# Values and gates in the heads take all 16 K tiles by Strassen

## The chip, the cores and the metric

The program runs on one core of a Trainium2 chip. The metric is the device time of one execution in microseconds. A core has TensorE (PE in the rows; its weight loads are PEld), VectorE (DVE), ScalarE (ACT), GpSimd (POOL) and SyncE (SP), which here issues the loads of weights.

## The reference

Two layers of a decoder trunk are applied to 512 prompt rows and 8 sample rows, 520 columns in all once the activations are transposed. The projection `h @ w_in` is where the change lies:

```python
h = rmsnorm(x, norm_g)
z = h @ w_in                                   # 2048 x 8192
b_c, c_c, x_c, g_c, q, k, v, g_r = split_projection(z)
...
o, new_S = retention(q, k, v, ret_S, retention_log_gamma())   # 4 heads of 256
y_ret = (groupnorm(o) * gn_g) * jax.nn.silu(g_r)
x = x + jnp.concatenate([y_conv, y_ret], axis=-1) @ w_out
x = x + jax.nn.sigmoid(x @ w_pg) * (p_i @ w_ple)
```

## The kernel before

Activations lie transposed: 16 K tiles of 128 rows by 520 columns, in two halves of 260. Every product is made in three matmuls of the fp32r type (`mm3`, lines 247 to 249): operands and weights are each split into a high and a low part, and high x high, high x low and low x high are added up. For weights `split_w` makes the high part on ScalarE (line 229) and the low part on VectorE (line 230); they lie in a ring of 60 tiles of 128 columns (`split`).

Output tiles are made in pairs, `pair(x, src, m, n)`, two tiles of 128 rows by 520 columns. A pair is the four blocks (two weight rows by two column halves), and `strassen` makes it with seven products instead of eight. It takes the first s of the 16 K tiles in two groups of s/2: the even tiles and the odd ones. Products use either the weights w11, w21, w22, w12 themselves or sums of them. The four sums are formed in place in the raw ring on VectorE (`add`, line 319), in chunks of up to 4 tiles (`CHA = 4`), and every product's weights are split in chunks of up to 4 tiles (`CHS = 4`). Loads of whole groups are line 312. The sums on the operands' side are made once for a layer and kept in slots (`x.sums`); a pair of s tiles uses the first s/2 of them.

K tiles beyond s are done plainly, at the end of the pair, in the loop `for i, j in chunks(s, KT)`: they are loaded and split by `parts` (loads at line 222), and each takes four products. With s = 14 there are two such tiles; with s = 16 none. Accumulators are PSUM banks `ps_g`, five in all. With s = 14 a pair takes a, b, c, d; with s = 16 the bank c is not taken, and one product is copied to the result's slot at once (`c = banks.get() if s < KT else None`). Copies and sums out of the banks are line 307, on ScalarE and VectorE; the copies `ps_g<-ps_g` go from bank to bank, two in a pair of 14 and one in a pair of 16.

The numbers s stand in tables, one entry per pair: `HEADS` (four pairs per head: queries q, keys k, values v, gates g), `CONVS` (16 pairs of the convolution branch, 14 in the first two and the last, else 16), `OUT_ROWS` and `GATES` for the two later products. In layer 0 the first head's q and k pairs are made elsewhere, so `HEADS[0][2:]` begins with its v pair. The host packs each pair's weights in the order that its s asks for (`k_order`), even tiles, odd tiles, the rest.

The work of a head's retention (scores, state, normalization) is cut in steps and put into the middle and the ends of the next head's pairs (`later`, `aside`), and the sample rows' state updates (`sample`) too. Those, the rope of q and k (lines 752 to 757) and the gates' silu are VectorE and ScalarE work beside the pairs. The final order on each engine is set by a scheduler that goes by a timeline of its own (`schedule_with_timeline_sim=True`) and by the priorities in the code.

Of the kernel before, what the change touches and what calls it, by code (L numbers as in the profile page):

```python
# [49 lines left out]
EARLY = 6  # L50


HEADS = [[0, 0, 0, 8] + [14] * 12, [0] + [14] * 15]
CONVS = [[14] * 2 + [16] * 13 + [14]] * 2
OUT_ROWS = [[0, 8, 16, 16, 16, 16, 16, 0]] * 2

# [135 lines left out]
def trunk_kernel(  # L192
# [370 lines left out]
    def norm_g(l, k):  # L563
        return vec[:, 16 * l + k : 16 * l + k + 1]
# [97 lines left out]
    def from_dram(src):  # L662
        def load(k):
            t = get()
            SIDE.dma_start(t, src[k])
            return t

        return load

    xs = []  # L670
    X = Operands(HEADS[0][2:] + CONVS[0], from_dram(xT), gain=lambda k: norm_g(0, k))
    X.todo = [t for t in ((i, False, True) for i in range(max(X.rows) // 2))]
# [43 lines left out]
    for l in range(DEPTH):  # L716
# [456 lines left out]
        if not tail:  # L1173
            X = Operands(HEADS[l + 1] + CONVS[l + 1], next_in, RESERVE_NEXT, gain=lambda k, l=l: norm_g(l + 1, k))
        for m in range(0, KT - tail, 2):
# [303 lines left out]
```

## Time and profile before

| | |
|---|---|
| time, median of 3 runs | 2168.64 us (2165.82 to 2170.73) |
| the profiled execution | 2169.1 us |
| its span | 2167.3 us |
| TensorE busy | 2147.8 us (99%), 17861 matmuls |
| VectorE busy | 1896.1 us (87%), 3849 instructions |
| ScalarE busy | 1264.5 us (58%), 2647 instructions |

The span is the profiled execution without 1.8 us around it. Matmuls overlap, so the length of one is longer than the time from one start to the next. On a line of a table of stretches, "(x..)" is the number of an engine's instructions in the stretch. The heads of layer 0 lie before about 381 us, the convolution pairs up to about 730 us; the heads of layer 1 lie between about 1110 and 1473 us, the convolution pairs up to about 1796 us. Within the heads 239 to 287 us holds a v and a g pair of layer 0 (head 2), 287 to 331 us a q and a k pair (head 3); 1379 to 1426 us holds a q and a k pair of layer 1 (head 3), 1426 to 1473 us the v and the g pair behind it.

### The profile page before, as it was taken

To read this page: it belongs to the slowest core of one execution; us is meant where nothing else is said; L and a number is where in the kernel's file an instruction comes from. 1 tells how busy PE (TensorE), PEld (TensorE's weight loads), DVE (VectorE), ACT (ScalarE), POOL (GpSimd) and SP (SyncE) were. 2 spreads that over 40 slices of the span, in tenths; PEclk is the share of its full clock that TensorE was granted. 3 is DMA by queue.
4 is the path that set the end of the run, shared out by engine and by line. 5 is a ranking of instruction groups with operands and counts; after the bars stand their busy time and mean duration, and the time that the engine had idled before them with its cause. 6 is when DMAs were issued, how large, how long until landed. Compare 5 with 4: busy or idle time off the path is not lost. (4 is left out here: it accounts for less than half of the span.)

```text
span 2167.3 us, 48178 instructions
## 1 busy us (share of the span) xinstructions
PE 2147.8 (99%) x17861; PEld 2142.1 (99%) x17861; DVE 1896.1 (87%) x3849; ACT 1264.5 (58%) x2647; POOL 430.6 (20%) x746
## 2 busy tenths in 40 slices
PE   9999999999999999999999999999999999999998
PEld 9999999999999999999999999999999999999998
DVE  8889988998999987987997988989999998879884
ACT  8656655565555655655765655565645555456565
POOL 2313222211001211200212222231111022011011
PEclk9999999999999999999999999999999999999999
DMA  8555565545543745645645566664464355566455
GB/s 288 171 175 197 181 217 184 178 157 175 158 129 118 238 156 187 215 154 160 215 144 175 172 213 191 189 209 170 151 182 149 120 158 202 176 207 200 128 164 198
DMA packets 182861, 387.31 MB, mean 179 GB/s; under 512 B 25888, under 2 KB 56352, under 8 KB 182624
## 3 DMA queue, kind: packets, MB, share of 16 engines
q1 hardware_dynamic: 128704, 212.98, 31.6%
q0 software_dynamic: 53056, 169.84, 23.8%
q8 instruction: 140, 2.29, 0.4%
q10 hardware_dynamic: 864, 1.39, 0.2%
q14 instruction: 97, 0.79, 0.1%
HBM read 318.96 MB, written 65.15 MB: 177 GB/s over the span
## 5 line engine op out<-in xcount | busy, mean ns | idle before, releaser
L247 PE MATMUL ps_g<-slot,split 128*128 128x260 f32 x5465 | 1531.6, 284 | 7.2 <-ACT slot L307 2.9
L248 PE MATMUL ps_g<-slot,split 128*128 128x260 f32 x5465 | 1534.3, 282 | 0.3 <-DVE slot L555 0.3
L249 PE MATMUL ps_g<-slot,split 128*128 128x260 f32 x5461 | 1519.9, 283 | 0.5 <-DVE split L230 0.5
L229 ACT ACTIVATE split<-raw 128x512 fp32r<-128x512 f32 (+2 forms) x1347 | 777.3, 596 | 583.1 <-DVE raw L319 213.2
L247 PEld LDWEIGHTS ps_g<-slot,split 128*128 128x128 f32 x5465 | 1024.0, 188 | 10.1 <-ACT slot L307 3.7
L248 PEld LDWEIGHTS ps_g<-slot,split 128*128 128x128 f32 x5465 | 1028.5, 188 | 0.5 <-DVE slot L555 0.5
L249 PEld LDWEIGHTS ps_g<-slot,split 128*128 128x128 f32 x5461 | 1019.8, 188 | 1.0 <-DVE split L230 1.0
L230 DVE TENSOR_TENSOR split<-raw,split 128x512 fp32r<-128x512 f32 (+2 forms) x1346 | 849.2, 652 | 172.5 <-PE ps_g L248 85.4
L319 DVE TENSOR_TENSOR raw<-raw 128x512 f32<-128x512 f32 (+1 forms) x660 | 428.9, 660 | 32.5 <-DMA raw<-wi 23.7
L307 ACT ACTIVATE slot<-ps_g 128x260 f32<-128x260 f32 x336 | 127.4, 381 | 140.6 <-PE ps_g L249 122.7
L551 ACT ACTIVATE slot<-slot 128x520 fp32r<-128x520 f32 (+1 forms) x212 | 109.2, 562 | 46.6 <-DVE slot L414 11.1
L552 DVE TENSOR_TENSOR slot<-slot,slot 128x520 fp32r<-128x520 f32 (+1 forms) x212 | 124.4, 620 | 4.1 <-ACT slot L551 3.9
L781 POOL DMA_DIRECT2D o_rets<-slot x64 | 35.3, 552 | 351.6 <-DVE slot L780 131.7
L307 DVE TENSOR_TENSOR slot<-ps_g,slot 128x260 f32<-128x260 f32 x168 | 70.9, 424 | 6.0 <-PE ps_g L249 3.7
L869 POOL DMA_DIRECT2D slot<-hs x64 | 46.2, 724 | 118.7 <-DVE split L230 42.7
L814 POOL DMA_DIRECT2D hs<-slot x64 | 35.6, 556 | 139.3 <-DVE slot L755 61.3
L780 DVE SCALAR_TENSOR_TENSOR slot<-slot,vs,slot 128x256 f32<-128x256 f32 x128 | 56.1, 481 | 4.5 <-ACT slot L776 4.3
L746 DVE TENSOR_TENSOR slot<-slot,slot 128x520 f32<-128x520 f32 x80 | 55.8, 698 | 4.7 <-DMA o_rets<-slot 3.7
L770 POOL DMA_DIRECT2D slot<-sret x64 | 35.5, 554 | 114.6 <-ACT split L229 37.3
L1058 POOL DMA_DIRECT2D slot<-x1s x76 | 40.8, 538 | 87.6 <-PE ps_g L249 27.2
L1209 POOL DMA_DIRECT2D x2s<-slot x30 | 16.4, 545 | 201.6 <-DVE slot L1204 200.6
L771 POOL DMA_DIRECT2D slot<-kq x64 | 34.9, 547 | 106.0 <-DVE slot L876 22.2
(217 smaller groups left out, 1733.8 us busy)
## 6 DMA issues: line engine op xcount, KB each, us to landing
raw<-wi SPq DMA_DIRECT2D x377, 256.0 KB, 3.9
raw<-wo SPq DMA_DIRECT2D x128, 256.0 KB, 5.4
raw<-wg SPq DMA_DIRECT2D x122, 256.0 KB, 4.1
raw<-wi SPq DMA_DIRECT2D x136, 192.0 KB, 4.0
slot<-x1s POOLq DMA_DIRECT2D x76, 260.0 KB, 5.1
slot<-sret POOLq DMA_DIRECT2D x64, 256.0 KB, 4.0
hs<-slot POOLq DMA_DIRECT2D x64, 256.0 KB, 4.0
slot<-hs POOLq DMA_DIRECT2D x64, 256.0 KB, 5.2
```

The costliest lines, as they stand in the source:

```text
L229: S.activation(hi, raw, AF.Copy)
L230: V.tensor_tensor(lo, raw, F(hi), SUB)
L247: PE.matmul(out, wh, xh, start=start, stop=False, skip_group_check=more)
L248: PE.matmul(out, wh, xl, start=False, stop=False, skip_group_check=more)
L249: PE.matmul(out, wl, xh, start=False, stop=stop, skip_group_check=more)
L307: fn(*args)
L319: V.tensor_tensor(out[:, n], x[:, n], y[:, n], op)
L551: keep(S.activation(hi, src[:, n], AF.Copy))
L552: V.tensor_tensor(lo, src[:, n], F(hi), SUB)
L746: V.tensor_tensor(out[:, n], v, table[:, n], MUL)
L780: keep(V.scalar_tensor_tensor(st[:, c], k, vs[:, h, e, b : b + 1], st[:, c], MUL, ADD))
L869: SIDE.dma_start(t[:, :512].rearrange("p (m n) -> p m n", m=2), src)
```

## The change

```diff
-HEADS = [[0, 0, 0, 8] + [14] * 12, [0] + [14] * 15]
+HEADS = [[0, 0, 0, 8] + [14, 14, 16, 16] * 3, [0, 14, 16, 16] + [14, 14, 16, 16] * 3]
```

In each group of four entries the first two are q and k, the last two v and g. The v and g pairs of heads 1 to 3 in layer 0 and of all four heads in layer 1 take s = 16 instead of 14: six pairs and eight. Each of them loses the loop over the two remaining tiles and the bank c, and its seven products and four weight sums have 8 tiles instead of 7. Numbers of instructions that differ in the whole program: TensorE 17827 to 17785; VectorE 3851 to 3823 (line 230: 98 splits of 128x384 become 128x512 and 28 of 128x256 go; line 319: 56 sums of 128x384 become 128x512); ScalarE 2655 to 2613 (line 229 as line 230, and 14 bank-to-bank copies go); SP 886 to 858 (28 loads of 128x256 go, 56 of 128x384 become 128x512).

VectorE, layer 0, the start of the same v pair, the difference: `split` and `raw` are weights, the rest is head 0's retention and head 1's rope.

```order
 L757 TENSOR_TENSOR slot_144_1422<-slot_144_1422,slot_164_1701 128x520
-L230 TENSOR_TENSOR split<-raw,split 128x384
+L230 TENSOR_TENSOR split<-raw,split 128x512
 L904 TENSOR_TENSOR slot_167_1850<-ps_s,slot_145_1542 128x512
-L319 TENSOR_TENSOR raw<-raw 128x384
+L319 TENSOR_TENSOR raw<-raw 128x512
 L918 SCALAR_TENSOR_TENSOR slot_173_1873<-ps_vt,r5p,slot_172_1872 128x256
-L230 TENSOR_TENSOR split<-raw,split 128x512
-L319 TENSOR_TENSOR raw<-raw 128x384
+L319 TENSOR_TENSOR raw<-raw 128x512
+L230 TENSOR_TENSOR split<-raw,split 128x512
 L876 TENSOR_TENSOR slot_169_1853<-slot_167_1850,slot_168_1852 128x512
```

Splits and sums of 3 tiles have become 4 tiles wide, and a sum stands before a split where it stood behind it.

TensorE, layer 0, the same v pair towards its end, with buffer numbers: before, `ps_g_2078`, `ps_g_2079` and `ps_g_2080` are its banks b, d and c, and the slots 46 to 49 hold the two remaining tiles.

```order
L248 MATMUL ps_g_2078<-slot44_45_577,split_73 128x260
L249 MATMUL ps_g_2078<-slot43_44_576,split_73 128x260
L247 MATMUL ps_g_2080<-slot46_47_605,split_73 128x260
L248 MATMUL ps_g_2080<-slot46_47_605,split_73 128x260
L249 MATMUL ps_g_2080<-slot46_47_605,split_73 128x260
L247 MATMUL ps_g_2080<-slot47_48_634,split_73 128x260
L248 MATMUL ps_g_2080<-slot48_49_635,split_73 128x260
L249 MATMUL ps_g_2080<-slot47_48_634,split_73 128x260
L247 MATMUL ps_g_2079<-slot45_46_604,split_73 128x260
L248 MATMUL ps_g_2079<-slot45_46_604,split_73 128x260
L249 MATMUL ps_g_2079<-slot45_46_604,split_73 128x260
```

The same pair now, where its fourth product (bank d) ends and the fifth begins; `ps_g_2077` is its bank a, `ps_g_2379` the first bank of the g pair behind it, and `ps_ot` is head 0's retention.

```order
L247 MATMUL ps_g_2079<-slot47_48_634,split_73 128x260
L248 MATMUL ps_g_2079<-slot48_49_635,split_73 128x260
L249 MATMUL ps_g_2079<-slot47_48_634,split_73 128x260
L995 MATMUL ps_ot_2214<-ident_75,slot13_179_2040 128x128 x4
L247 MATMUL ps_g_2379<-slot2_3_119,split_73 128x260
L248 MATMUL ps_g_2379<-slot2_3_119,split_73 128x260
L247 MATMUL ps_g_2077<-slot52_79_777,split_73 128x260
L248 MATMUL ps_g_2077<-slot53_80_778,split_73 128x260
L249 MATMUL ps_g_2077<-slot52_79_777,split_73 128x260
L247 MATMUL ps_g_2077<-slot1_91_941,split_73 128x260
```

The matmuls of the remaining tiles are gone. The g pair's first product is begun ahead of the v pair's fifth product; before, it stood ahead of the last 27 matmuls into bank a.

## Rows read from the trace of the kernel before

**Rows 1.** The page's head: the span; busy time and share of each engine.

```profile
span 2167.3 us, 48178 instructions
...
PE 2147.8 (99%) x17861; PEld 2142.1 (99%) x17861; DVE 1896.1 (87%) x3849; ACT 1264.5 (58%) x2647; POOL 430.6 (20%) x746
```

**Rows 2.** Timeline of TensorE in layer 0's heads: start, length (us), instruction.

```profile
300.12 0.28 PE L247 MATMUL ps_g<-slot,split 128*128 128x260 f32 x1
300.24 0.28 PE L248 MATMUL ps_g<-slot,split 128*128 128x260 f32 x1
300.36 0.28 PE L249 MATMUL ps_g<-slot,split 128*128 128x260 f32 x1
```

**Rows 3.** Stretches: length, busy us (x instructions) by engine, granted clock, DMA share, GB/s.

```profile
500.00:700.00 200.00, 200.00 (x1672) 200.00 (x1671) 181.12 (x359) 106.14 (x213) 23.30 (x32) 1.00 0.48 144
150.00:380.00 230.00, 230.00 (x1925) 230.00 (x1924) 206.98 (x467) 136.66 (x303) 67.02 (x115) 1.00 0.63 198
...
239.00:287.00 48.00, 48.00 (x404) 48.00 (x403) 43.70 (x100) 29.19 (x64) 15.29 (x26) 1.00 0.63 196
287.00:331.00 44.00, 44.00 (x369) 44.00 (x369) 40.17 (x90) 26.20 (x58) 11.94 (x22) 1.00 0.66 205
...
535.00:645.00 110.00, 110.00 (x919) 110.00 (x919) 102.85 (x199) 60.61 (x122) 8.69 (x16) 1.00 0.45 136
645.00:745.00 100.00, 96.68 (x803) 96.07 (x802) 93.10 (x195) 59.42 (x138) 21.92 (x31) 1.00 0.55 175
...
1379.00:1426.00 47.00, 46.79 (x392) 46.59 (x391) 44.44 (x98) 26.39 (x61) 12.35 (x22) 1.00 0.62 186
1426.00:1473.00 47.00, 46.54 (x390) 46.34 (x389) 39.61 (x95) 28.80 (x65) 11.50 (x19) 1.00 0.63 195
...
1710.00:1800.00 90.00, 87.96 (x728) 87.12 (x728) 86.31 (x180) 56.21 (x129) 17.64 (x23) 1.00 0.53 172
```

**Rows 4.** Groups of instructions by shape, whole span: xcount | busy us, mean ns | idle before.

```profile
L230 DVE TENSOR_TENSOR split<-raw,split 128x512 fp32r<-128x512 f32 x1031 | 695.0, 690 | 147.8 <-PE ps_g L248 81.2 <-ACT split L229 51.8 <-issue 6.1
...
L229 ACT ACTIVATE split<-raw 128x512 fp32r<-128x512 f32 x1032 | 632.3, 626 | 462.3 <-DVE raw L319 188.2 <-PE ps_g L249 166.4 <-PE ps_g L248 45.1
...
L319 DVE TENSOR_TENSOR raw<-raw 128x512 f32<-128x512 f32 x520 | 354.1, 688 | 17.6 <-DMA raw<-wi 12.1 <-DMA raw<-wo 2.9
...
L230 DVE TENSOR_TENSOR split<-raw,split 128x384 fp32r<-128x384 f32 x249 | 137.1, 555 | 16.2 <-ACT split L229 9.9 <-PE ps_g L248 3.4 <-ACT slot L551 1.9
...
L229 ACT ACTIVATE split<-raw 128x384 fp32r<-128x384 f32 x249 | 127.2, 518 | 84.0 <-DVE raw L319 25.0 <-PE ps_g L248 24.2 <-PE ps_g L249 17.9
...
L319 DVE TENSOR_TENSOR raw<-raw 128x384 f32<-128x384 f32 x140 | 77.4, 554 | 14.9 <-DMA raw<-wi 11.6 <-DMA raw<-wg 2.8
...
L307 ACT ACTIVATE ps_g<-ps_g 128x260 f32<-128x260 f32 x121 | 45.1, 373 | 16.4 <-PE ps_g L249 16.1
...
L230 DVE TENSOR_TENSOR split<-raw,split 128x256 fp32r<-128x256 f32 x66 | 27.3, 423 | 8.5 <-ACT split L229 7.6 <-PE ps_g L248 0.8
...
L229 ACT ACTIVATE split<-raw 128x256 fp32r<-128x256 f32 x66 | 27.3, 415 | 36.7 <-DMA raw<-wi 29.0 <-PE ps_g L248 5.2 <-PE ps_g L249 1.9
```

**Rows 5.** Waits of TensorE, whole span: us in total, times, longest us.

```profile
PE ps_g L247 <- ACT slot L307: 2.9, 4, 1.3
PE ps_g L247 <- ACT ps_g L307: 1.6, 2, 1.2
PE ps_g L247 <- ACT split L229: 1.5, 2, 1.3
PE warm L657 <- POOL half_neg L596: 1.1, 1, 1.1
```

**Rows 6.** Waits of VectorE between 100 and 490 us.

```profile
DVE split L230 <- PE ps_g L248: 8.2, 14, 1.5
DVE split L230 <- ACT split L229: 6.2, 10, 1.4
DVE raw L319 <- DMA raw<-wi: 4.8, 4, 2.5
```

## The prediction

> **What bounds the kernel now.** I read the page's first part, then TensorE in order of time, then a table of stretches. The page has TensorE busy 99% of the span, VectorE 87%, ScalarE 58% [rows 1]. A busy share of pipelined matmuls proves little, so I looked at starts: inside a head a 128x260 matmul starts every 0.12 us and none of them waits [rows 2]. Over 230 us of layer 0's heads 1925 matmuls start, one per 0.1195 us; over 200 us of the convolution pairs 1672 start, one per 0.1196 us [rows 3]. Both stretches are without idle time on TensorE, and the granted clock is 1.00, the 2.4 GHz level, in every stretch. All that TensorE waits for work comes to a few us: the four largest entries of its waits are 2.9, 1.6, 1.5 and 1.1 us of 2167.3 [rows 5]. So time is the number of matmuls times their spacing, as long as the engines that feed TensorE keep their lead.
>
> The feeder that is short is VectorE. It makes the low half of every split weight and all sums of weights, and it does so in order with the rope, gate and sample work. In the heads I cut the trace at the two bank-to-bank copies of each 14-tile pair. They cost little, and the fullest stretch of a v and a g pair is 239 to 287 us, VectorE busy 43.70 of 48 (91.0%); the least full that I show is 1426 to 1473 us, 39.61 of 47 (84.3%). Stretches of q and k pairs are fuller: 40.17 of 44 (91.3%) and 44.44 of 47 (94.6%) [rows 3]. The changed pairs are thus those with more room on VectorE. And it is ahead: between 100 and 490 us its longest-summed wait is for TensorE to free weight tiles, 8.2 us in 14 waits [rows 6].
>
> **The change part by part.**
>
> TensorE. A pair that takes s tiles by Strassen has 7 products of s/2 tiles and 4 products for each remaining tile, with 3 matmuls per tile and product: 14 tiles give 147 + 24 = 171, 16 tiles give 168. Six pairs change in layer 0 and eight in layer 1: 14 x 3 = 42 matmuls fewer, and the two programs differ on TensorE by just these. Price: 0.1195 us each from the 230 us stretch [rows 3], not the 284 ns that the page gives as the length of one, since they overlap. 42 x 0.1195 = 5.0 us, all on the path, because TensorE has no idle time in these stretches to take it up. The bounds are the start-to-start times that the timeline shows, 0.12 us, and nothing at all, if TensorE waited in their place.
>
> The Trainium skill, page "TensorE: Matmul & The Clock Gate", section "Back-to-back issue gap", has N/2.4 + 2.5 ns for a warm matmul, 110.8 ns for 260 columns. By it the sum would be an estimated 4.7 us instead of 5.0. The trace's spacing is wider, 119.5 ns, and I use that.
>
> VectorE. Per changed pair, each of the 7 products' chunks of 3 tiles becomes one of 4, each of the 4 sums likewise, and the two splits of the remaining 2 tiles go. With the lengths of [rows 4]: 7 x (0.690 - 0.555) + 4 x (0.688 - 0.554) - 2 x 0.423 = 0.945 + 0.536 - 0.846 = +0.64 us per pair, 14 x 0.64 = +8.9 us in all. It lies beside TensorE's work: the two pairs of a stretch add 1.3 us to VectorE while TensorE needs 0.7 us less. The stretch at 239 us goes from 43.70/48 to 45.0/47.3, 95%; that at 1426 us from 39.61/47 to 40.9/46.3, 88%. The q and k pair behind it stays at 91 to 95%. Is 95% too much? The nearest rows say no: between 535 and 645 us, in pairs of 16 tiles, VectorE is busy 102.85 of 110 (93.5%) and TensorE is not idle once; between 1379 and 1426 us it is 94.6%, with 0.2 us of TensorE's time lost [rows 3]. If the cover is gone, a matmul waits for its low half and what VectorE lacks is paid in full.
>
> ScalarE. 7 x (0.626 - 0.518) - 2 x 0.415 - 0.373 = 0.756 - 0.830 - 0.373 = -0.45 us per pair; the last term is a bank-to-bank copy that a 16-tile pair doesn't make [rows 4]. ScalarE is 58% busy [rows 1], so this is worth nothing by itself, but it is the releaser of 2.9 and 1.6 us of TensorE's waits [rows 5].
>
> Loads. The same weight bytes come in fewer, larger transfers, 28 fewer on SP. The remaining-tile loads no longer take raw regions between two pairs, so the next pair's first load can start a product earlier; against that, the 24 matmuls without sums at a pair's end (24 x 0.1195 = 2.9 us), during which VectorE has only two splits to make, no longer pad the end. I take the two as equal. Nothing moves in the operand sums: the eighth sum of each layer is already built before the pairs that now read it, in layer 0 before head 1's k pair and in layer 1 before head 0's v pair. Slots are taken and freed at the same places.
>
> Scheduling. The order of all engines in the heads is redone. In layer 0's head 1 TensorE now begins the g pair's first product, which needs no sums, ahead of the v pair's fifth product instead of its last one. VectorE's order differs again for 115 and 160 instructions at the borders from convolution to output pairs. There the trace of before loses 100.00 - 96.68 = 3.3 us (645 to 745 us) and 90.00 - 87.96 = 2.0 us (1710 to 1800 us) [rows 3]. A new order can win or lose some of this; I take zero and 2 us either way for the range.
>
> Sum: -5.0 on TensorE, +0.2 for a wait such as that between 1379 and 1426 us, -4.8 us. Against the profiled execution, whose own time is 2169.1 us, that is 2164.3. That execution is 0.5 us over the runs' median of 2168.64, so the forecast is 2168.64 - 4.8 = **2163.8 us**.
>
> **The rivals.**
>
> (B) *VectorE's lead runs thin now and then.* The two pairs of a stretch take 1.3 + 0.7 = 2.0 us of its lead. If the q and k pairs, at 91 to 95%, cannot rebuild it, a low half is late somewhere in most changed pairs. Price: the 0.2 us stretch at 1379 us is the nearest, a wait of 0.5 us at 1426 us (47 - 46.54) the next; 0.25 us in each of 14 pairs is 3.5 us and leaves 2168.64 - 5.0 + 3.5 = 2167.1. For it: 95% is over every stretch that runs clean. Against it: 93.5% runs clean for 110 us, and layer 1's stretches have more room.
>
> (C) *VectorE becomes the bound, and the kernel is slower.* From 239 to 331 us VectorE has 92 - 83.87 = 8.1 us of idle time per head. If that could not shrink (it waits for ScalarE's high halves, for weights, for landed stores), each head would take VectorE's own 0.64 us per pair: 8.9 us more instead of 5.0 less, 2177.5. It decides where idle time per head cannot go under 8.1 us, 9% of the stretch. Against it: from 535 to 645 us only 6.5% is idle and TensorE runs on; after the change 92 - 0.7 = 91.3 us hold 85.1 of work, 6.8% idle.
>
> (D) *The borders are redone well.* The convolution borders give back 2 us of their 5.3: 2161.8. Nothing in the order shows the sign.
>
> (E) *Evictions in too few banks.* A 16-tile pair holds three accumulators, a 14-tile pair four, and one is reused for four products, each after a copy by ScalarE. If each changed pair met one wait of 1.3 us, the longest for such a copy [rows 5], the cost would be 14 x 1.3 = 18.2 us: 2168.64 - 5.0 + 18.2 = 2181.8. Against it: from 535 to 645 us all pairs are such pairs, and TensorE is busy 110.00 of 110 [rows 3].
>
> On (E), the Trainium skill, page "Perfetto Trace Analysis", section "Optimizing Tensor Performance", asks that independent groups rotate through different banks so that evacuation overlaps the next group. By that rule the step from four banks to three would speak against the change; the 110 us stretch doesn't bear it out.
>
> That the change does nothing is excluded by the count of instructions.
>
> **How the numbers follow.** Forecast 0.62 (2162.4 to 2165.2, by how waits in the stretches fall), B 0.22, D 0.10, C 0.03, E 0.03. A difference of 0.2%, 4.3 us, is about what a measurement of this kernel can tell from no change: it puts the line at 2164.3, within my forecast's own spread. Two thirds of the forecast (0.42), D, and a little of B are faster: 0.54. The rest of the forecast and nearly all of B are within it: 0.40. C, E lie on the slow side: 0.06. The range takes in the forecast, D with its 2 us and a little for the scatter of the runs, and B: 2160.5 to 2168.5.
>
> **What would show it.** 42 matmuls fewer at an unchanged spacing near 0.1195 us; VectorE's busy time up by about 9 us, ScalarE's down by about 6; the v and g stretches shorter by 0.7 us each, with VectorE at 88 to 95% there. B would show as waits of TensorE for line 230's splits in the heads, C as VectorE near 100% with gaps on TensorE, E as waits for line 307 within changed pairs, D as a different loss at the two borders. I am wrong if the spacing rises in the heads, or if the q and k pairs, not the changed ones, begin to wait.

## The result and the profile after

The changed kernel is slower: 2178.5 us (median of 5 runs, 2177.66 to 2183.34) against 2169.24 us for the kernel before in the same session, a ratio of 1.0048, interval 1.0037 to 1.0059. That is 9.3 us more, where 4.8 us less was forecast, and 10 us above the upper end of the range. The profiled execution took 2178.0 us, its span 8.9 us more than in [rows 1]:

```profile
span 2176.2 us, 47932 instructions
...
PE 2148.6 (99%) x17819; PEld 2141.0 (98%) x17819; DVE 1906.1 (88%) x3821; ACT 1264.2 (58%) x2605; POOL 431.7 (20%) x746
```

TensorE has its 42 matmuls fewer, VectorE 10.0 us more to do. In stretches without idle time the spacing is unchanged: 110 us hold 920 matmuls between 535 and 645 us (919 in [rows 3]). So the 5.0 us were gained, and some 14 us were lost elsewhere (8.9 + 5.0). The waits of TensorE over the whole span, as in [rows 5] (us in total, times, longest):

```profile
PE ps_g L247 <- ACT slot L307: 10.6, 8, 3.6
PE ps_g L249 <- DVE split L230: 3.4, 4, 2.3
PE ps_g L247 <- ACT split L229: 1.5, 2, 1.3
PE ps_g L247 <- DVE slot L307: 1.1, 1, 1.1
```

ScalarE's copies out of banks (line 307) went from 2.9 us to 10.6, VectorE's low halves (line 230) from 0.5 to 3.4. Of these, 0.6 + 6.6 = 7.2 us and 2.3 + 0.4 = 2.7 us lie in the heads; the rest lies at the borders and behind them, among it one wait of 2.46 us for a copy at 1803.66 us. The stretches of the heads, first layer 0, then layer 1; after:

```profile
100.00:381.00 281.00, 277.99 (x2304) 277.17 (x2304) 253.33 (x546) 163.47 (x348) 76.42 (x131) 0.99 0.60 190
...
1110.00:1473.00 363.00, 354.27 (x2927) 351.48 (x2926) 320.04 (x670) 205.35 (x437) 90.69 (x155) 1.00 0.57 183
```

and the same two stretches of the kernel before:

```profile
100.00:381.00 281.00, 281.00 (x2352) 281.00 (x2351) 254.23 (x567) 168.42 (x371) 77.19 (x133) 1.00 0.60 190
1110.00:1473.00 363.00, 361.93 (x3018) 360.74 (x3017) 320.03 (x701) 210.66 (x472) 91.25 (x157) 1.00 0.60 186
```

TensorE is idle for 3.0 and 8.7 us, before for 0 and 1.1: 10.6 us more. With some 3 us of slower clock behind two stalls (last section) that makes up nearly all of the 13.9 us. VectorE is busy for the same time in the same length: 320.03 and 320.04 us of 363. It has the changed pairs' extra work to do, and the 43 us in which it is idle did not shrink to make room for it.

The two longest stalls show how. The first is in layer 0, head 2 (rows of TensorE, VectorE, ScalarE and of the loads that SP issues, in order of time):

```profile
249.25 0.33 SPq L312 DMA_DIRECT2D raw<-wi  x1
...
252.13 0.69 DVE L756 TENSOR_TENSOR slot<-slot,slot 128x520 f32<-128x520 f32 x1
252.74 1.89 DVE L230 TENSOR_TENSOR split<-raw,split 128x512 fp32r<-128x512 f32 x3
253.94 0.63 ACT L229 ACTIVATE split<-raw 128x512 fp32r<-128x512 f32 x1 [3.07 <-DMA raw<-wi]
254.55 0.42 DVE L784 CUSTOM_DVE_ANT_0 slot<-slot,slot 128x256 f32<-128x256 f32 x1
254.89 0.69 DVE L230 TENSOR_TENSOR split<-raw,split 128x512 fp32r<-128x512 f32 x1
255.64 0.50 PE L249 MATMUL ps_g<-slot,split 128*128 128x260 f32 x1 [2.31 <-DVE split L230]
```

Read it from the end. The matmul at 255.64 waits 2.31 us for the low half made at 254.89; that needs the high half of 253.94, and that waits for weights whose load is issued only at 249.25 and takes 4.6 us (the median of the loads issued there). The load in its turn waits for VectorE to have read the raw region that it overwrites, which the waits of SP between 239 and 262 us show:

```profile
SPq L312 <- DVE split L230: 12.0, 5, 8.8
SPq L312 <- DVE raw L319: 10.7, 2, 9.5
```

VectorE's last operation that ended before 249.25 is a weight sum (line 319), at 249.22. And VectorE comes to it from a full queue: 8.00 us busy of 8.00 between 245 and 253 us (stretches, columns as in [rows 3]):

```profile
245.00:253.00 8.00, 8.00 (x69) 8.00 (x68) 8.00 (x16) 4.16 (x8) 1.58 (x3) 1.00 0.49 146
253.00:256.00 3.00, 0.69 (x5) 0.48 (x4) 3.00 (x7) 0.73 (x2) 2.22 (x4) 0.96 0.94 314
256.00:260.00 4.00, 4.00 (x23) 4.00 (x23) 3.44 (x12) 2.16 (x6) 2.26 (x5) 0.60 0.86 253
260.00:264.00 4.00, 4.00 (x36) 4.00 (x35) 3.53 (x6) 1.54 (x3) 1.49 (x3) 1.00 0.57 213
```

The first row by itself is no stall. In the same 8 us the kernel before has VectorE just as full, and TensorE runs on:

```profile
245.00:253.00 8.00, 8.00 (x69) 8.00 (x68) 8.00 (x21) 3.16 (x8) 4.38 (x7) 1.00 0.85 251
```

What differs is which operations VectorE does in them, and with that when the loads go out: the mean busy share of the DMA engines is 0.85 there before, and after it is 0.49, then 0.94 in the 3 us behind. Lateness of VectorE thus comes back one load later. The second stall is in layer 1, head 2, and goes through ScalarE:

```profile
1329.17 0.70 DVE L757 TENSOR_TENSOR slot<-slot,slot 128x520 f32<-128x520 f32 x1
1329.90 0.21 ACT L838 ACTIVATE qks<-slot 128x8 f32<-128x8 f32 x1 [3.16 <-DVE slot L757]
1330.45 0.41 DVE L784 CUSTOM_DVE_ANT_0 slot<-slot,slot 128x256 f32<-128x256 f32 x1
1330.95 0.95 ACT L307 ACTIVATE slot<-ps_g 128x260 f32<-128x260 f32 x3 [0.85 <-DVE osum L784]
1331.39 0.58 PE L247 MATMUL ps_g<-slot,split 128*128 128x260 f32 x1 [3.60 <-ACT slot L307]
```

TensorE can't begin a product of the v pair until ScalarE has copied its bank. The copy stands in ScalarE's queue behind an 8-column copy of k (line 838), which waits 3.16 us for the last operation of k's rope on VectorE (line 757), and then waits itself for a sample reduction there (line 784), the last reader of the slot that it writes. No weight split is made on ScalarE in this time either.

### The profile page after: what moved, and what is told of

Read it like the earlier page. It is cut to its first block, busy times and chain, and to the rows that moved or that the text cites. A ratio compares the mean times of both kernels' runs of the same rounds, so it can differ in the third digit from the quotient of the medians.

```text
span 2176.2 us, 47932 instructions
## 1 busy us (share of the span) xinstructions
PE 2148.6 (99%) x17819; PEld 2141.0 (98%) x17819; DVE 1906.1 (88%) x3821; ACT 1264.2 (58%) x2605; POOL 431.7 (20%) x746
## 4 chain that ended last, share of the span: by engine, by line
PE 85%; DVE 6%; DMA 4%; issue 3%; ACT 1%; SPq 0%; POOL 0%; DVEq 0%; POOLq 0%; ACTq 0%
PE ps_g L247 26%; PE ps_g L249 26%; PE ps_g L248 26%; DMA raw<-wi 3%; DVE split L230 2%; DVE raw L319 1%; DMA o_rets<-slot 1%; ACT split L229 1%; PE ps_p L247 0%; PE ps_p L249 0%; PE ps_p L248 0%; DVE slot L552 0%; DMA x2s<-slot 0%; DVE slot L780 0%; PE ps_s L249 0%
## 5 line engine op out<-in xcount | busy, mean ns | idle before, releaser
L247 PE MATMUL ps_g<-slot,split 128*128 128x260 f32 x5451 | 1530.5, 284 | 14.5 <-ACT slot L307 10.6
L229 ACT ACTIVATE split<-raw 128x512 fp32r<-128x512 f32 (+2 forms) x1319 | 779.1, 608 | 600.1 <-DVE raw L319 246.6
L319 DVE TENSOR_TENSOR raw<-raw 128x512 f32<-128x512 f32 (+1 forms) x660 | 434.9, 669 | 32.7 <-DMA raw<-wi 29.0
```

The lines of the kernel that those rows point to most:

```text
L229: S.activation(hi, raw, AF.Copy)
L247: PE.matmul(out, wh, xh, start=start, stop=False, skip_group_check=more)
L319: V.tensor_tensor(out[:, n], x[:, n], y[:, n], op)
```

## The experiments

The candidates were: the eviction out of three banks instead of four, with one copy straight into a slot (the prediction's E); VectorE's added work (B and C); the new order of the heads, whatever the work; and single places, such as the copy of line 838. Differences in us are medians against the kernel before in the same session. "Idle" is TensorE's, the length less the busy time in 100 to 381 us and 1110 to 1473 us together; it doesn't hold the slower clock after a stall.

**Banks and slots.** The first kernel gives 16-tile head pairs the fourth bank back, with the copy into it, the other two exchange the order in which the two result slots are taken (of the changed kernel, and of the kernel before):

```diff
-        c = banks.get() if s < KT else None
+        c = banks.get() if s < KT or spare else None
```

> The 16-tile pairs of the heads keep a fourth accumulator bank as the 14-tile pairs do, so the second product is copied from bank to bank and the result's second slot is first written after the fifth product. Matmuls stay 42 fewer than before, ScalarE makes 14 + 14 copies more. Theory S (ScalarE copies a result early into a slot whose last reader is not done, and holds the copies behind it, so TensorE waits for banks): about 2165 us, the waits of TensorE for line 307's ScalarE copies in the heads from 7 us to under 1. Theory V (VectorE's lead is used up by its 0.64 us more per pair): about 2178, as the changed kernel.

Measured: +18.9 us, ratio 1.0083 (1.0065 to 1.0100), idle 15.4. The longest entry of TensorE's waits is still line 307:

```profile
PE ps_g L247 <- ACT slot L307: 9.7, 9, 2.6
```

In the heads alone these waits are 5.8 us (7.2 in the changed kernel). The bank does not cure them; but this kernel too has another order of the heads, so what the bank is worth by itself is not shown.

```diff
-        z0, z1 = get(), get()
+        z1, z0 = get(), get()
```

> The kernel before (all tables as before), with the two result slots of every Strassen pair taken in the other order, so the work is the same to the instruction and only dependences on old slots move; the scheduler then orders both layers' heads anew and leaves convolutions as they were. Theory O (the order that the scheduler happens to give in the heads decides, and that of before is a good one): 2173 to 2185 us, waits of TensorE in the heads of several us. Theory W (the work of the changed pairs decides): 2168, as before.

> The changed kernel with the two result slots taken in the other order, so the slot that the second product is copied to early is the one freed longer ago. Theory S (early copies wait for a slot's last reader): about 2167. Theory O: another draw, 2170 to 2187. Theory V (VectorE's totals): 2178.

Measured: in the kernel before +16.4 us, ratio 1.0071 (1.0056 to 1.0086), idle 7.8, at exactly the same work on every engine; in the changed one +30.7, 1.0140 (1.0125 to 1.0156), idle 24.3. The exchange gives a pair's halves slots with other last readers, and it draws all orders anew; the runs don't separate the two. The kernel before with exchanged slots waits for line 307 for 4.4 us in its heads (0.2 before), so these waits are no property of 16 tiles.

**Some of the pairs.** Only the values, only the gates, only the first changed pair (layer 0, head 1, v), only layer 0's six:

```diff
-HEADS = [[0, 0, 0, 8] + [14, 14, 16, 16] * 3, [0, 14, 16, 16] + [14, 14, 16, 16] * 3]
+HEADS = [[0, 0, 0, 8] + [14, 14, 16, 14] * 3, [0, 14, 16, 14] + [14, 14, 16, 14] * 3]
...
+HEADS = [[0, 0, 0, 8] + [14, 14, 14, 16] * 3, [0, 14, 14, 16] + [14, 14, 14, 16] * 3]
...
+HEADS = [[0, 0, 0, 8] + [14, 14, 16, 14] + [14] * 8, [0] + [14] * 15]
...
+HEADS = [[0, 0, 0, 8] + [14, 14, 16, 16] * 3, [0] + [14] * 15]
```

> Of the changed pairs only the values take 16 tiles, seven pairs, 21 matmuls fewer than before. The changed kernel's long waits (253, 1143, 1238 and 1327 us) lie where a v pair starts beside the rope of k. If the place counts (S, or V by the burst of rope): about 2175, nearly the whole loss. If the mere sum of VectorE's work counts (V by totals): about half of the loss, 2173.

> Of the changed pairs only the gates take 16 tiles, seven pairs, 21 matmuls fewer than before. If the place counts: faster than before by up to 2.5 us, 2167. If totals of VectorE count: about 2173.

> The kernel before with one single pair changed to 16 tiles, the values of head 1 in layer 0: 3 matmuls fewer, VectorE 0.64 us more. The heads behind it, layer 1's too, hold the work of before in another order. Theory O: 2173 to 2185, with the losses far from the changed pair. Theory W: 2167 to 2169.

> Only layer 0's six pairs take 16 tiles; layer 1's heads have the work of before, in another order. Theory O: TensorE waits in layer 1's heads too (1.0 us before, then some 5 us), 2172 or more in all. Theory W: layer 1's heads lose nothing, layer 0's lose what the changed kernel lost there, about 5 us less the 2.2 us of matmuls: 2171.

Measured: values alone +12.4 us (1.0058, 1.0041 to 1.0075), gates alone +15.7 (1.0068, 1.0053 to 1.0083), the first pair +0.8 (1.0007, 0.9997 to 1.0017), layer 0's six +5.4 (1.0021, 1.0012 to 1.0031). Half of the pairs cost as much as all of them or more, so the loss is no sum over pairs; and the gates, which a loss tied to the start of the v pairs would have spared, cost no less than the values. One pair alone is not clear of no change, against the 2173 us and more that was expected of a new order, though its profile has TensorE idle for 4.8 us in layer 1's heads. With only layer 0 changed, TensorE is idle for 5.3 us in layer 1's heads, whose work is that of the kernel before (before: 1.1):

```profile
1110.00:1473.00 363.00, 357.73 (x2958) 355.35 (x2957) 313.48 (x686) 207.07 (x463) 91.82 (x156) 1.00 0.59 185
```

An edit in one head re-orders the instructions of all later heads, and the order alone is worth some us of idle time there.

**A null change, and VectorE's work at 14 tiles.** To price the order, a VectorE operation that changes nothing was put into the v and g pairs: 8 columns wide for the order alone, 512 columns (0.69 us) for order and work. In the first pair of kernels it stands ahead of the fourth product, in the second ahead of the seventh (on w22):

```diff
         add(w21, w12, w21, SUB)
+        if spare:
+            with tc.high_priority(offset=WPRIO):
+                V.tensor_tensor(w12[:, :8], w12[:, :8], w12[:, :8], ALU.max)
```

> The kernel before (14 tiles) with a VectorE instruction of 128x8 more in the v and g pairs' fourth weight (15 pairs; it leaves the values as they are): some 0.1 us of VectorE per pair, 1.5 in all, the same matmuls, another order in the heads. Theory O (a new order costs by itself): 2172 to 2178, waits in layer 1's heads 4 us or more against 1.0 before. Theory V (VectorE's added work is what costs): 2168 to 2169.

> The same with 128x512 in place of 128x8: 0.69 us of VectorE per pair, as much as the change adds, at the same matmuls as before. Theory V: before plus the 14 us that the change lost against its matmuls, 2180. Theory O: as the run with 128x8, 2172 to 2178.

> The kernel before with the 128x8 VectorE instruction at another weight (w22, ahead of the seventh product) of the 15 v and g pairs: the work of before, a third new order of the heads. Theory O alone: again 2172 to 2178. If VectorE's load is the larger part: 2169 to 2174, since the two orders drawn so far cost 1 and 8 us.

> The same place, 128x512: 0.69 us of VectorE per pair. Theory V: 4 to 10 us over the run with 128x8 at this place, some 2178 to 2182. Theory O alone: no more than that run, within 3 us.

Measured: ahead of the fourth product 8 columns cost 7.7 us (1.0030, 1.0016 to 1.0044; idle 7.2), 512 columns 12.2 (1.0049, 1.0033 to 1.0066; idle 10.2); ahead of the seventh 1.8 (1.0004, 0.9995 to 1.0013; idle 3.5) and 5.1 (1.0025, 1.0016 to 1.0034; idle 4.4). So a null change costs up to 8 us (7.7 in one place, 1.8 and not clear of zero in the other), and the exchanged slots cost 16.4: the kernel before has a good order. The wide operation keeps VectorE busy for 6.6 us more than the narrow one in both places (1905.0 against 1898.4, 1903.2 against 1896.6), and the kernels with it are 4.5 and 3.2 us slower. That points to work that is not hidden, though TensorE's work is unchanged and VectorE's share of the span stays at 87 to 88%. It does not prove it: the wide kernels have yet another order than the narrow ones (VectorE's differs in over 100 places in the heads), and 3 to 5 us is less than an order can cost.

**VectorE's work at 16 tiles.** The fourth weight sum of the changed pairs is left out, 14 x 2 x 0.688 = 19.3 us; and the null change of 8 columns on either kernel, ahead of the fourth product with the sum, ahead of the seventh without it:

```diff
-        add(w21, w12, w21, SUB)
+        if not (spare and s == KT):
+            add(w21, w12, w21, SUB)
```

> The changed kernel without the fourth weight sum in the 14 pairs, so a wrong weight goes into one product: VectorE does 2 x 0.688 us less per pair, less than in the 14-tile pair of before, at the same matmuls, copies and slots. Theory V: about 2164. Theory S: about 2176, the waits for line 307 stay.

> The changed kernel with the 128x8 instruction, another order of the same work. Theory O alone: anywhere between 2164 and 2187, and not worse on the whole than the 14-tile kernel with it. Theory V: 2178 to 2181.

> The changed kernel without the fourth weight sum in the changed pairs (a wrong weight in one product, as in the first run of this kind), with the 128x8 instruction: less VectorE work than before, another order. Theory V: near the first such run, 2166 to 2172. Theory O alone: like the other orders of the changed kernel, 2178 to 2187.

Measured: without the sum +0.4 us (1.0006, 0.9996 to 1.0016; idle 5.5), without the sum and with the null change +1.9 (1.0007, 0.9998 to 1.0017; idle 6.8); the changed kernel with the null change +17.6 (1.0076, 1.0061 to 1.0091; idle 13.1), without it +9.3 (idle 11.7). Without this work the kernels are 8.9 us faster, and 15.7 with the null changes, whose places and orders differ. These are the largest differences here that go with VectorE's work, but the sixth product's weights are the removed sum (`times(b, w21, ...)`), so leaving it out shortens a chain as well as a queue, and every one of these kernels has its own order. And it wins nothing: with VectorE at 1892.7 us, 3.4 under the kernel before, and 42 matmuls fewer, the time is that of before.

**16 tiles at VectorE's old work.** Only the second half of that sum is left out, 9.6 us, which is about what the change adds:

```diff
-        add(w21, w12, w21, SUB)
+        if spare and s == KT:
+            with tc.high_priority(offset=WPRIO):
+                V.tensor_tensor(w21[:, :512], w12[:, :512], w21[:, :512], SUB)
+        else:
+            add(w21, w12, w21, SUB)
```

> The changed kernel without the second chunk (128x512) of the fourth weight sum in the changed pairs (a wrong weight in half of one product): VectorE does 0.69 us less per pair, so as much as before to within 0.05 us per pair, at 42 matmuls fewer. If VectorE's work is the whole systematic loss: 2164 to 2171, as the 14-tile kernels with the 128x8 instruction (2170 and 2176) less 5 us. If 16-tile pairs cost something of their own: 2172 to 2180.

> The same with the 128x8 instruction, another order. The same two expectations; the two runs' distance tells how far one order is from another.

Measured: +5.9 us (1.0025, 1.0016 to 1.0035; VectorE 1898.9, idle 7.8), with the null change (ahead of the seventh product) +11.9 (1.0047, 1.0030 to 1.0065; VectorE 1901.1, idle 13.9). At nearly equal VectorE work (1896.1 to 1898.4) the kernels with 14 tiles in all of these pairs, or all but one, lie at 0, +0.8, +1.8, +7.7 and, with exchanged slots, +16.4, and they have 5 us more of matmuls to do. Both kernels here lie within that scatter, so a cost of the 16-tile pair besides VectorE's work is neither shown nor excluded. Over the last three groups of runs all six comparisons have the kernel with less VectorE work ahead: by 3.2 and 4.5 us where VectorE is busy for 6.6 us less, by 3.4 and 5.7 for 7.2 and 5.4 us, by 8.9 and 15.7 for 13.4 and 14.5. Each holds a new order; together they make VectorE's work a likely part of the loss.

**Two single places.** The 8-column copies of k (line 838) on GpSimd instead of ScalarE, and the fourth sum of the changed pairs on GpSimd instead of VectorE:

```diff
-                S.activation(qks[:, 2 + d, :NS], kf[d][:, SEQ:T], AF.Copy)
+                G.tensor_copy(qks[:, 2 + d, :NS], kf[d][:, SEQ:T])
...
-        add(w21, w12, w21, SUB)
+        if spare and s == KT:
+            for i, j in chunks(0, q, CHA):
+                n = slice(P * i, P * j)
+                G.tensor_tensor(w21[:, n], w12[:, n], w21[:, n], SUB)
+        else:
+            add(w21, w12, w21, SUB)
```

> The changed kernel with the two small copies of the rope's k (128x8 for the sample rows) on GpSimd instead of ScalarE, so ScalarE's copies out of the banks no longer stand behind a copy that waits for VectorE's rope. Theory S' (ScalarE's in-order queue, held by that copy, is where the v pairs lose): the waits at the v pairs (1144, 1331 us) go, about 5 us: 2173. Theory O: another draw, 2174 to 2187.

> The changed kernel with all its sums, the fourth one of the changed pairs on GpSimd instead of VectorE: VectorE has 1.38 us less per pair, GpSimd some 3 us more. Theory V: 2164 to 2170, the one version that could beat before. If GpSimd's sums come late, a new wait stands in for the old one: 2175 or more, with TensorE or VectorE waiting for GpSimd's raw tiles.

Measured: the copies moved, +15.6 us (1.0076, 1.0058 to 1.0093; idle 13.2). The stall in head 2 of layer 1 is still there. ScalarE now comes to the copies at once and waits for the reduction alone; so line 838 did not hold it, VectorE's lateness did:

```profile
1334.43 0.41 DVE L784 CUSTOM_DVE_ANT_0 slot<-slot,slot 128x256 f32<-128x256 f32 x1
1334.93 0.95 ACT L307 ACTIVATE slot<-ps_g 128x260 f32<-128x260 f32 x3 [4.70 <-DVE osum L784]
1335.37 0.39 PE L247 MATMUL ps_g<-slot,split 128*128 128x260 f32 x1 [3.09 <-ACT slot L307]
```

And a longer one has come in head 0: the transpose behind the moved copies holds VectorE's queue.

```profile
1148.06 0.31 DVE L841 STREAM_TRANSPOSE qkt<-qks 128x128 f32<-128x128 f32 x1 [7.36 <-POOL qks L838]
...
1150.20 0.58 PE L249 MATMUL ps_g<-slot,split 128*128 128x260 f32 x1 [4.83 <-DVE split L230]
```

The sums on GpSimd, +25.8 us (1.0113, 1.0096 to 1.0130; idle 21.6). The group of its 28 sums (busy us, mean ns):

```profile
L354 POOL TENSOR_TENSOR raw<-raw 128x512 f32<-128x512 f32 x28 | 48.5, 1733 | 28.4 <-DVE split L230 27.8 <-DVE mv L986 0.4
```

1733 ns against 688 on VectorE [rows 4]: 28 x 1045 = 29 us more for the same sums, with the sixth product's weights behind them. Nor does VectorE have less to do. Its busy time is 1915.9 us against 1906.1 in the changed kernel, though the 28 sums are gone: 16 of its 128x512 splits and sums in the heads took over 1000 ns, each while a GpSimd sum ran, 19.3 us more in all than at their median of 684 ns; in the changed kernel none took so long. One of them, at layer 0:

```profile
145.03 1.67 POOL L354 TENSOR_TENSOR raw<-raw 128x512 f32<-128x512 f32 x1 [3.51 <-DVE split L230]
145.46 1.78 DVE L319 TENSOR_TENSOR raw<-raw 128x512 f32<-128x512 f32 x1
```

So this run does not tell what less work on VectorE would bring. No kernel tried is shown to beat the one before.

## Why the prediction was wrong

**TensorE, -5.0 us: right.** 42 matmuls fewer at the unchanged spacing.

**VectorE, +8.9 us beside TensorE's work: this step failed.** Its size was right (+10.0 measured over the span), its cover was not. I took 93.5% in the convolution pairs, clean for 110 us, as proof that 95% would run clean in the heads. But there 80.2 of VectorE's 102.85 us are splits and sums of weights (lines 230 and 319, 78%); at 239 to 287 us they are 28.2 of 43.70 (65%), with more rope, sample and normalization work between them. A share does not say whether a split or a load comes in time: VectorE is full for the same 8 us at 245 us before and after, without a stall and with one. In the heads TensorE was idle for 11.7 us in place of 1.1. The runs make it likely that the added work costs time: with 13 to 15 us less of it at 16 tiles the kernels are 9 to 16 us faster, with 6.6 us more at 14 tiles 3 to 5 slower. How much is the work and how much the order is not shown.

The reading that the changed pairs have more room on VectorE was wrong for layer 1, where eight of the 14 pairs lie. The stretches that I took there are off by one pair. Head 3's rope of k, which follows its k pair, ends in the copies of line 838 at 1411.8 and 1416.1 us, where its v pair has begun, as head 2's do in layer 0 at 248.4 and 251.4 us. So 1379 to 1426 us holds the k and the v pair, and 1426 to 1473 us the g pair and the first convolution pair; the heads' own pairs end near 1450 us. Cut between pairs, the q and k pairs of head 3 and the v and g pairs behind them are:

```profile
1355.00:1402.00 47.00, 46.79 (x391) 46.59 (x391) 41.86 (x98) 26.18 (x60) 12.77 (x23) 1.00 0.66 202
1402.00:1450.00 48.00, 48.00 (x404) 48.00 (x403) 43.70 (x101) 29.06 (x65) 14.15 (x24) 1.00 0.62 187
```

That is 89.1% for q and k and 91.0% for v and g; in heads 1 and 2 it is 87.7 and 90.2% against 89.9 and 88.7%. The 94.6% stretch has a v pair in it, and the 84.3% one has only one pair that was changed.

**Rivals B and C: in part the right mechanism, B priced at 0.25 us per pair, C given a chance of 0.03.** The waits for line 230 in the heads that were to show B are there, 2.7 us in two waits; but most of the waiting there, 7.2 us in six, is for ScalarE's copies, and in the longest of these (3.6 us) the copy waits for VectorE. I had looked for B only in the splits. C gave 2177.5, near the measured time, and its condition, VectorE's idle time per head doesn't shrink, is what layer 1 shows (320.03 and 320.04 of 363). That isn't the whole of it, and its near number is in part luck: by C the kernels with the sum left out (VectorE 1892.7 and 1892.0) should be 3 to 4 us under the kernel before and those with the halved sum 3 to 5 above, and they lie 0.4 and 1.9, and 5.9 and 11.9, above it.

**ScalarE, worth nothing by itself: wrong in kind.** Its work fell by 0.3 us, not by 6: the bank-to-bank copies by 5.2 as computed (45.1 to 39.9), but line 229's busy time rose by 1.8 (777.3 to 779.1) where I had -1.0, and the rest is in groups too small to follow. What counts is whom its queue waits for. Its waits for weight sums in layer 1's heads (1130 to 1473 us) went from 27.8 us to 51.7:

```profile
ACT split L229 <- DVE raw L319: 51.7, 39, 3.9
...
ACT qks L838 <- DVE slot L757: 5.3, 4, 3.2
```

**Loads, taken as equal: right in the sum, wrong at places.** VectorE's waits for loads of weights in 1110 to 1473 us are 14.7 us before and 14.4 after. But a load starts when VectorE has done with the region, so a late VectorE means late loads (the stall at 255 us), and behind a 16-tile g pair, without the 24 matmuls whose weights need no sums, the q pair's weights come late. Layer 1, head 1:

```profile
1188.80 0.56 DVE L319 TENSOR_TENSOR raw<-raw 128x384 f32<-128x384 f32 x1 [3.63 <-DMA raw<-wi]
...
1191.38 0.39 PE L247 MATMUL ps_g<-slot,split 128*128 128x260 f32 x1 [1.16 <-ACT slot L307]
```

That these 24 matmuls were the place where VectorE caught up is argued from the code and this wait; no run put them back alone.

**Scheduling, zero with 2 us either way at the borders: wrong place and size.** The two borders lost 2.3 (645 to 745 us) and 2.9 us (1710 to 1805 us) after, 3.3 and 2.0 before [rows 3]: as forecast, and without the gain of D. The order in the heads was given no price: it was put at nothing without a reason. The null changes put it at up to 8 us, the exchanged slots at 16, and there was nothing to win, since in the two stretches of heads above the kernel before is idle for just 1.1 us.

**Rival E: right line, wrong cause.** TensorE's longest waits are for line 307, and at least four of them, 5.5 of the 10.6 us, lie within changed pairs, which I had said would show E. The fourth bank didn't help, and such waits come as well at 14 tiles (4.4 us in the heads of the kernel before with its slots exchanged, 8.5 in all). Whether other slots for the early copies would take these waits away wasn't tried.

What stays open: how the 13.9 us divide. A new order at the work of before cost from nothing that is clear of zero to 16 us, less work on VectorE went with a gain of 3 to 16 us, and the work was never varied without the order; a cost of the 16-tile pair itself is not shown. The Trainium skill's page "Perfetto Trace Analysis", section "Identifying the Most-Contended Engine", takes the occupancy of VectorE as a fair measure of how close it is to its limit; here it rose by one point, 87 to 88%, and the time was lost, and in the slower kernel with exchanged slots at 14 tiles it is 87% as before.

## What to carry to other kernels

A busy share of 90% over a stretch does not say how much more work an engine that works in order can take. Nor does a stretch of a few us where it is full: the same 8 us were full with and without a stall. Ask which split, copy or load stands behind the full queue, and who waits for it, on that engine and on those that feed from it. Cover proven in one stage is no proof for another with other work beside it. Where a scheduler redoes the order, run a null change first: an effect smaller than what that costs can't be laid on the edit by one comparison.

## What was not expected of the hardware

Behind the two stalls above TensorE runs on the lower level for some us. The stretch 256 to 260 us above has the granted clock at 0.60 and 23 matmuls, the next 4 us 1.00 and 36. The same behind the second stall, of 3.6 us:

```profile
1328.00:1331.50 3.50, 0.11 (x1) 0.11 (x1) 3.39 (x13) 0.76 (x3) 2.19 (x5) 0.92 0.84 258
1331.50:1335.00 3.50, 3.50 (x19) 3.50 (x20) 2.73 (x5) 2.09 (x5) 3.20 (x5) 0.59 0.95 306
1335.00:1339.00 4.00, 4.00 (x36) 4.00 (x35) 2.79 (x7) 1.26 (x2) 0.00 (x0) 1.00 0.37 140
```

At the lower, 1.2 GHz level a matmul starts every 0.22 us:

```profile
256.15 0.42 PE L248 MATMUL ps_g<-slot,split 128*128 128x260 f32 x1
256.37 0.42 PE L249 MATMUL ps_g<-slot,split 128*128 128x260 f32 x1
256.59 0.42 PE L247 MATMUL ps_g<-slot,split 128*128 128x260 f32 x1
```

So a stall of 2.3 us cost 36 - 23 = 13 matmuls more, 13 x 0.1195 = 1.6 us, and one of 3.6 us about as much. The prediction's prices per wait didn't have this. But not every stall did it. Behind the wait of 2.46 us at the border of layer 1, longer than the first, the granted clock is 1.00 with 36 matmuls in 4 us:

```profile
1803.66 0.39 PE L247 MATMUL ps_g<-slot,split 128*128 128x260 f32 x1 [2.46 <-ACT slot L307]
1804.00:1808.00 4.00, 4.00 (x36) 4.00 (x35) 4.00 (x10) 2.08 (x6) 1.07 (x2) 1.00 1.04 387
```

The Trainium skill, page "TensorE: Matmul & The Clock Gate", Part 1, knows these two levels and has the clock fall when TensorE has been idle. The two stalls shown agree with that; the third shows that a wait of this length does not always lower it.
